# Moving the S5 units of a hybrid layer ahead, into the key/value projection

## The chip, the cores and the metric

The kernel runs on one core of a Trainium2 chip. The metric is device time in microseconds (us) from one execution of the whole program; the number quoted for a kernel is the median over its runs. The engines are named as the profile names them: PE (matrix multiply; PEld is its weight load), DVE (vector), ACT (scalar and activation), POOL (GpSimd), and SP, whose queue here issues nearly all loads. Each engine works through its own instructions in the order in which the program wrote them.

## The reference

Two layers of a diffusion backbone over 256 context and 256 latent tokens, width 1024. Each layer is a half-step SwiGLU, a token mixer, and a second half-step SwiGLU. The case is about the mixer of layer 0, which runs two head groups on the same input: a bidirectional S5 state-space group and a grouped-query attention group.

```python
def mixer_ab(hx, hc, ...):
    z = hx @ w_in
    u, q, k, v = jnp.split(z, [S5_WIDTH, S5_WIDTH + qw, S5_WIDTH + qw + kw], axis=-1)
    ...
    for r in range(2):                     # forward and reversed
        yl, yc = s5_direction(uc, u, ...)  # linear recurrence over tokens, then a read-out
        y_lat = y_lat + yl
    ...
    b_lat = dense_gqa(qn, kn, v, kcn, vch) # latent queries read 512 keys
    b_ctx = attend_full(qc, kcn, vch)      # context queries read 256 keys
    out_lat = jnp.concatenate([s5_glu(y_lat, glu_w), b_lat], axis=-1) @ w_out
```

## The kernel before

All matrix work is float32 by three products: a weight or activation is split into a high part (`whi`, `hh`: a cast) and a low part (`wlo`, `hl`: a subtraction), and `mm3` (lines 350 to 352) multiplies high by high, high by low and low by high. The split of a weight block is two casts on ACT (line 252) and two subtractions on DVE (line 258).

**Loads.** A list `plan` holds every weight block in the order of use. `fetch` issues them on the SP queue into a ring of three buffers `raw` of 1 MB. For a weight (`"w"`) the buffer is given back when its low part is written; for S5 data (`"s"`) when the S5 unit that reads it calls `done_raw`. Before the change the order around the mixer is: key/value weights `abkv`, the two halves of the query weights `abq`, then the S5 blocks `at` (input matrices, one for two units) and `me` (read-out matrices) in order of use. `u_load` brings the S5 input `U` back from DRAM in two halves of eight transfers each; `s5_tab` loads a unit's rotation table `tbl` (256 KB) into one of three buffers.

**The mixer (`mixer_ab`)** runs these stages on PE: the projection to S5 inputs (`puu`), four blocks of 128 tokens of keys and values (`pkv`, line 1575 on), four blocks of queries in two halves (`pq`), attention, then the output projection (`pwo`). After every piece of PE work the code calls `tick()`, which takes one step of each generator in the list `bg`: `k_gen` and `q_gen` finish a block of keys or queries (norm, rotary table, transposes), and `s5_gen` runs the events that are due at its tick number. Thus a tick number is a place in the order of every engine's instructions. Before the change `s5_gen` enters `bg` after the key/value blocks, so its tick 0 lies in the first half of query block 0.

**The S5 work** is eight units n = 0 to 7 (quad n // 2 and direction n % 2). A unit is issued at tick `S5_TICKS[n]`: 32 small matmuls `psS` on PE (line 1415) and a copy `Ssb` on ACT (line 1418; one buffer, `SB = 1`). One tick later come two rotations on POOL (lines 1443 to 1445, three operations of 128x256 each, then a copy `rhoT`), which read `Ssb` and `tbl`. Three and four ticks after the issue come two halves of the scan on DVE: two scans (line 1460), then products `pr` and `t` (1469, 1470) and the states `H` (1474); the second half has no scans. Six and seven ticks after the second unit of a quad come the two read-out halves `py` on PE (line 1492), and a tick later a copy `yt` on ACT.

**Attention** has 16 score steps, numbered 0 to 15 here; each is two heads of 128 queries, against 256 keys in steps 0 to 7 and 512 in steps 8 to 15. A step is the scores `sc` on PE, the row maximum `mx` on DVE (line 893), the exponentials `P` on ACT (line 913), scaling on ACT (928) and POOL (930), and three steps later transposes `ppt` and their copies (941); the products with the values `po` follow every second step. Each step is one tick.

Of the kernel before, what the change touches and what calls it, by code (L numbers as in the profile page):

```python
# [21 lines left out]
KT = D // 128  # L22
# [14 lines left out]
def hybrid_kernel(ctx: ExitStack, tc: tile.TileContext, x, c, ctx_in, c_ctx, mod_w, mod_b, norm_g, ffn_wg, ffn_wu,  # L37
# [6 lines left out]
    def pool(name, bufs=1, **kw):  # L44
        return ctx.enter_context(tc.tile_pool(name=name, bufs=bufs, **kw))

    S5_TICKS = (0, 3, 7, 9, 12, 15, 17, 19)
    S5_LAG = (0, 3, 4, 6)
    QL = (1, 2, 2, 2)
    FK = (0, 1, 3, 6)  # L50
# [34 lines left out]
    FL = (1, 3)  # L85
    SPL = (1, 1, 1, 1)
    LT = 0
    GT = 3
    GN = 1
    AH = 26  # L90
    KL = ((3, 7), (1, 2), (2, 3), (1, 1))
    PB = (8, 6)
    TBB = 3
    SB = 1
    ctx.enter_context(tc.manual_schedule())
# [88 lines left out]
    bg = []  # L184
# [78 lines left out]
    def lo_done(i):  # L263
        while lo_q and lo_q[0][0] <= i:
            lo_q.pop(0)[1]()
# [27 lines left out]
    def use(key, pre=True, mods=True):  # L293
        if mods:
            run_mods()
        while plan[st["cur"]][0] == "s":
            st["cur"] += 1
        i = st["cur"]
        assert plan[i][1] == key, (plan[i][1], key)
        fetch()  # L300
        prep(i)
        lo_done(i)
        st["cur"] += 1
        if pre:
            ahead()
        return prepped.pop(i)

    def w_spec(key, w, r0, nr, c0, ncol):
        plan.append(("w", key, nr, ncol, lambda rv: [
            (rv, w[r0:r0 + nr * 128, c0:c0 + ncol].rearrange("(k p) n -> p k n", p=128))]))  # L310
# [532 lines left out]
    def k_gen(ap, psrc, nh, l, t, kTh, kTl, tok, lag=(1, 1)):  # L843
# [8 lines left out]
        for i0 in range(0, nh, 2):  # L852
            hl = ap.tile([128, 2, 4, 64], F32R, name="khl", tag="P", bufs=PB[l])
            yy = y[:, i0:i0 + 2, None, :].to_broadcast([128, 2, 2, 64])
# [465 lines left out]
    def ab_specs():  # L1320
        w = ab_w_in[0]
        for i in range(2):
            w_spec(("abu", i), w, 0, KT, 256 * i, 256)
            for ch in (range(MA), range(MA, 4))[i]:
                m_spec(0, 6, ch)
        o = [(("abkv",), w, 0, KT, 1024, 256)]
        o += [(("abq", i), w, 512 * i, 4, 512, 512) for i in range(2)]
        for sp in o:
            w_spec(*sp)

        def at_spec(qd):
            plan.append(("s", ("at", qd), 2, 1024, lambda rv: [(rv, at_d[qd])]))

        def me_spec(i):
            plan.append(("s", ("me", i), 12, 128, lambda rv: [
                (rv.rearrange("p (f g) n -> p f (g n)", f=2),
                 me_d[i // 2][:, :, i % 2].rearrange("p f b z n -> p f (b z n)"))]))

        def mx_spec(ch):
            plan.append(("s", ("mx", ch), 8, 256, lambda rv: [  # L1340
                (rv, mod_w[0, :, 7 * D + ch * 256:7 * D + (ch + 1) * 256].rearrange("(k p) n -> p k n", p=128))]))

        uses = [(S5_TICKS[2 * qd], 0, at_spec, qd) for qd in range(4)]
        uses += [(S5_TICKS[2 * (i // 2) + 1] + S5_LAG[3] + i % 2, 1, me_spec, i) for i in range(8)]
        uses += [(t, 2, mx_spec, ch) for ch, t in enumerate(MX)]
        for _, _, f, i in sorted(uses, key=lambda u: u[:2]):
            f(i)
        def wo_spec(kh, ch):
            def srcs(rv, cs_=slice(ch * 512, (ch + 1) * 512)):
                if kh == 0:  # L1350
                    return [(rv, w_out[0, 0:512, cs_].rearrange("(k p) n -> p k n", p=128))]
                return [(rv[64 * kvl:64 * kvl + 64],
                         w_out[0, 512 + 256 * kvl:768 + 256 * kvl, cs_].rearrange("(k p) n -> p k n", p=64))
                        for kvl in range(2)]
            plan.append(("w", ("wo0", kh, ch), 4, 512, srcs))

        wo_spec(1, 0)
        def glu_srcs(z):
            return lambda rv: [(rv[64 * qe:64 * qe + 64, 2 * qp:2 * qp + 2],
                                glu_w[0, z, 256 * qp + 128 * qe:256 * qp + 128 * qe + 128].rearrange("(a f) n -> f a n", a=2))  # L1360
                               for qp in range(2) for qe in range(2)]

        for z in range(2):
            plan.append(("w", ("glu", z), 4, 512, glu_srcs(z)))
        wo_spec(0, 0)
        wo_spec(1, 1)
        wo_spec(0, 1)

    def mixer_ab(nm, ap, nxt):
# [33 lines left out]
        def s5_tab(n):  # L1403
            qd, r = divmod(n, 2)
            tb = ap.tile([128, 2, 4, 64], F32, name="tbl", tag="tbl", bufs=TBB)
            nc.sync.dma_start(tb, tab_d[r][:, :, qd * 256:(qd + 1) * 256].rearrange("p z (q c) -> p z q c", q=4))
            return tb
# [16 lines left out]
        s5 = {"tb": {}, "sb": {}, "uu": {}, "H": {}, "py": {}}  # L1424
# [71 lines left out]
        def s5_store(qd):  # L1496
            qp, qe = divmod(qd, 2)
            if qe == 0:
                tg_ = ("qhl", "tbl")[qp]
                s5["yt", qp] = [ap.tile([128, 4, 2, 64], F32, name="yt", tag=tg_, bufs=(2, TBB)[qp]) for _ in range(2)]  # L1500
            py = s5["py"].pop(qd).rearrange("p (s j h) -> p s j h", s=4, j=8)
            for jh in range(2):
                S.copy(s5["yt", qp][jh][:, :, qe].rearrange("p j (s h) -> p s j h", h=16), py[:, :, 4 * jh:4 * jh + 4])
# [23 lines left out]
        def at_tick(t, f, *a):  # L1527
            events.setdefault(t, []).append(lambda: f(*a))

        TU = S5_TICKS  # L1530
        o_ = S5_LAG
# [11 lines left out]
        for n in range(8):  # L1543
            at_tick(TU[n], s5_unit, n)
        for n in range(8):
            at_tick(max(0, TU[n] - 2), lambda n: s5["tb"].update({n: s5_tab(n)}), n)
        def mod_raw(ch):
            mod_chunk((0, 7, -1 - ch), use_raw(("mx", ch)))
            done_raw()

        for ch, t in enumerate(MX):
            at_tick(t, mod_raw, ch)
        at_tick(AH, ahead)
        tg = TU[7] + o_[3] + GT
        for k in range(4):
            at_tick(tg + k // GN, gelu, k // 2, k % 2)

        def s5_gen():
            for t in range(max(events) + 1):
                for f in events.get(t, []):  # L1560
                    f()
                yield
# [7 lines left out]
        kTh = ap.tile([128, 2, 512], F32R, name="kTh")  # L1570
        kTl = ap.tile([128, 2, 512], F32R, name="kTl")
        v = ap.tile([128, 4, 128], F32, name="v")
        qT = ap.tile([128, 8, 512], F32R, name="qT", tag="big")
        ckv = use(("abkv",))
        for t in range(4):
            tk = slice(t * 128, (t + 1) * 128)
            pkv = ps("pkv")
            for k in range(KT):
                s_, tl = tokens(t)
                mm3(pkv[:, 0:256], (hh[:, s_, k, tl], hl[:, s_, k, tl]), (ckv[0][:, k], ckv[1][:, k]), k == 0, k == KT - 1)  # L1580
            S.copy(v[:, t], pkv[:, 128:256])
            bg.append(k_gen(ap, pkv[:, 0:128], 2, 0, t - 2 if t >= 2 else None, kTh, kTl, tk))
            tick()
            if t == 1:
                u_load(1)
        sg_ = s5_gen()
        bg.append(sg_)
        rq = ap.tile([128, 4, 2, 8], F32, name="rq")
        cqs = {}
        for t in range(4):  # L1590
# [344 lines left out]
```

## Time and profile before

| | us |
|---|---|
| median of 3 runs | 1775.09 |
| lowest and highest | 1774.59, 1776.67 |
| the profiled execution | 1775.49 |
| its span, first to last instruction | 1773.7 |
| PE busy in the span | 1720.3 |
| DVE busy | 1051.9 |
| ACT busy | 633.3 |
| POOL busy | 447.3 |

The span is nearly the whole time; 1.8 us lie around it. Over the program PE is busy for 97%. Only a short part of the span holds the change: the key/value and query projections from 478.6 us, attention from 521 us, and the output projection from 609.7 us. What bounds this part is read from its own stretch and not from the sums above.

### The profile page before, as it was taken

What the parts mean: (1) busy time and instruction counts of PE and PEld (TensorE: products, weight loads), DVE (VectorE), ACT (ScalarE), POOL (GpSimd) and SP (SyncE); (2) the same over time, 40 slices, a digit from 0 to 9 for tenths busy, and PEclk for the clock granted to TensorE, in tenths of its full rate; (3) what the DMA queues carried; (4) which work ended last, traced back from release to release, by engine and by line L of the source; (5) the groups of instructions that cost most, each with busy time, mean ns of one, the idle gap of its engine ahead of it and who ended that gap; (6) DMA issues with size and microseconds to landing.
All of it is one profiled execution on the core that took longest, in us unless ns stands there. A gap on an engine that the chain in (4) does not pass through costs nothing.

```text
span 1773.7 us, 25534 instructions
## 1 busy us (share of the span) xinstructions
PE 1720.3 (97%) x10127; PEld 1433.3 (81%) x10127; DVE 1051.9 (59%) x1760; ACT 633.3 (36%) x1202; POOL 447.3 (25%) x601
## 2 busy tenths in 40 slices
PE   6999999999987999999999999999999998999998
PEld 4778878878975789888888888888888876699998
DVE  5566767665579644576653355765644468755555
ACT  3322222223446634222222233222222347754443
POOL 5314768322467304000000032000000146630000
PEclk8999999999998899999999999999999999999999
DMA  8546475585444524564433325553524244155653
GB/s 265 184 136 178 147 216 172 184 286 190 159 144 157 137 83 137 167 210 136 147 113 101 119 99 182 171 167 130 158 78 133 95 167 96 40 199 167 198 181 121
DMA packets 209247, 272.63 MB, mean 154 GB/s; under 512 B 23464, under 2 KB 171176, under 8 KB 208616
## 3 DMA queue, kind: packets, MB, share of 16 engines
q1 hardware_dynamic: 203632, 257.06, 46.1%
q10 hardware_dynamic: 4136, 9.52, 1.5%
q0 software_dynamic: 1360, 4.42, 0.8%
q8 instruction: 80, 1.31, 0.3%
q14 instruction: 39, 0.32, 0.1%
HBM read 255.77 MB, written 15.17 MB: 153 GB/s over the span
## 4 chain that ended last, share of the span: by engine, by line
PE 81%; DVE 7%; DMA 4%; POOL 3%; ACT 2%; issue 2%; SPq 0%; POOLq 0%; ACTq 0%
PE pu L350 15%; PE pu L351 15%; PE pu L352 15%; PE pd L350 6%; PE pd L352 6%; PE pd L351 6%; PE pwo L350 1%; PE pwo L352 1%; PE pwo L351 1%; PE pacc L351 1%; PE pacc L350 1%; PE pacc L352 1%; DMA me_d<-Et 1%; PE pm L411 1%; DVE H L1474 1%
## 5 line engine op out<-in xcount | busy, mean ns | idle before, releaser
L350 PE MATMUL pu<-hh,whi 128*128 128x512 f32 (+1 forms) x1472 | 528.2, 359 | 1.3 <-ACT hh L505 1.1
L351 PE MATMUL pu<-hl,whi 128*128 128x512 f32 (+1 forms) x1472 | 523.5, 356 | 3.5 <-DVE hl L507 2.6
L352 PE MATMUL pu<-hh,wlo 128*128 128x512 f32 (+1 forms) x1472 | 522.8, 355 | 0.1
L258 DVE TENSOR_TENSOR wlo<-raw,whi 128x1024 fp32r<-128x1024 f32 (+2 forms) x326 | 370.5, 1176 | 62.1 <-ACT whi L252 61.7
L252 ACT CAST whi<-raw 128x1024 fp32r<-128x1024 f32 (+2 forms) x330 | 308.3, 984 | 275.4 <-PE pd L351 158.9
L350 PEld LDWEIGHTS pu<-hh,whi 128*128 128x128 f32 x1472 | 278.4, 189 | 51.6 <-issue 6.8
L351 PEld LDWEIGHTS pu<-hl,whi 128*128 128x128 f32 x1472 | 278.5, 189 | 43.0 <-DVE hl L507 3.4
L352 PEld LDWEIGHTS pu<-hh,wlo 128*128 128x128 f32 x1472 | 278.4, 189 | 40.0 <-DVE wlo L258 0.7
L462 POOL TENSOR_TENSOR acc<-acc,sq 128x256 f32<-128x256 f32 x54 | 43.1, 801 | 774.7 <-ACT sq L468 773.8
L350 PE MATMUL pd<-ahi,whi 128*128 128x512 f32 (+1 forms) x624 | 224.8, 360 | 0.3 <-ACT ahi L217 0.3
L351 PE MATMUL pd<-alo,whi 128*128 128x512 f32 (+1 forms) x624 | 222.7, 357 | 0.5 <-DVE alo L218 0.5
L555 DVE TENSOR_TENSOR hm<-sg,pu 128x512 f32<-128x512 f32 (+1 forms) x88 | 54.4, 618 | 284.1 <-PE pu L352 284.1
L352 PE MATMUL pd<-ahi,wlo 128*128 128x512 f32 (+1 forms) x624 | 222.6, 357 | 0.0
L217 ACT CAST ahi<-hm 128x512 fp32r<-128x512 f32 (+1 forms) x88 | 49.9, 567 | 362.6 <-DVE hm L555 362.6
L546 DVE SCALAR_TENSOR_TENSOR xT<-pd,m,xT 128x256 f32<-128x256 f32 x192 | 84.5, 478 | 104.4 <-PE pd L352 104.2
L350 PEld LDWEIGHTS pd<-ahi,whi 128*128 128x128 f32 x624 | 117.9, 189 | 20.6 <-issue 2.9
L352 PEld LDWEIGHTS pd<-ahi,wlo 128*128 128x128 f32 x624 | 117.9, 189 | 17.5 <-DVE wlo L258 0.5
L351 PEld LDWEIGHTS pd<-alo,whi 128*128 128x128 f32 x624 | 118.0, 189 | 17.3 <-DVE alo L218 0.8
L551 ACT ACTIVATE sg<-pu 128x512 f32<-128x512 f32 (+1 forms) x88 | 47.6, 544 | 224.2 <-PE pu L352 223.7
L441 DVE SCALAR_TENSOR_TENSOR ma<-mraw,silc,ma 128x1024 f32<-128x1024 f32 (+1 forms) x112 | 123.7, 1145 | 6.4 <-DMA mraw<-in_mod_w_dram 6.4
L218 DVE TENSOR_TENSOR alo<-hm,ahi 128x512 fp32r<-128x512 f32 (+1 forms) x88 | 56.0, 636 | 56.7 <-ACT ahi L217 56.7
L505 ACT ACTIVATE hh<-h,m 128x256 fp32r<-128x256 f32 x88 | 41.2, 502 | 58.8 <-DVE h L498 58.8
(355 smaller groups left out, 2328.1 us busy)
## 6 DMA issues: line engine op xcount, KB each, us to landing
raw<-in_ffn_wg_dram SPq DMA_DIRECT2D x44, 1024.0 KB, 5.4
raw<-in_ffn_wu_dram SPq DMA_DIRECT2D x44, 1024.0 KB, 5.5
raw<-in_mod_w_dram SPq DMA_DIRECT2D x40, 1024.0 KB, 5.0
raw<-in_ffn_wd_dram SPq DMA_DIRECT2D x36, 768.0 KB, 4.9
mraw<-in_mod_w_dram SPq DMA_DIRECT2D x48, 512.0 KB, 4.7
raw<-in_ffn_wd_dram SPq DMA_DIRECT2D x17, 1024.0 KB, 5.0
raw<-me_d SPq DMA_DIRECT2D x8, 768.0 KB, 5.5
raw<-in_win_w_in_dram SPq DMA_DIRECT2D x6, 1024.0 KB, 5.3
```

The costliest lines, as they stand in the source:

```text
L217: (S.copy if eng is None else eng.tensor_copy)(dst_hi, src)
L218: V.tensor_sub(dst_lo, src, dst_hi.bitcast(F32))
L252: S.copy(v[0][:, js], raw[:, js])
L258: eng.tensor_sub(v[1][:, js], raw[:, js], v[0][:, js].bitcast(F32))
L350: T.matmul(o, lhs[0], rhs[0], start=start, stop=False)
L351: T.matmul(o, lhs[0], rhs[1], start=False, stop=False)
L352: T.matmul(o, lhs[1], rhs[0], start=False, stop=stop)
L441: V.scalar_tensor_tensor(ma[c0, s_], raw[i], silc[:, k, s_:s_ + 1], ma[c0, s_], op0=OP.mult, op1=OP.add)
L462: G.tensor_add(acc[s_], acc[s_], sq_late.pop(s_))
L546: V.scalar_tensor_tensor(xT[:, d, sl], psrc, m[:, l, j, d, s_:s_ + 1], xT[:, d, sl], op0=OP.mult, op1=OP.add)
L551: S.activation(sg, pg, AF.Silu)
L555: V.tensor_mul(hm, sg, pu)
```

## The change

The S5 generator enters `bg` ahead of the key/value blocks. Its ticks 0 to 3 now lie in these blocks, ticks 4 to 12 in and behind the query projections, and the score steps begin at tick 13. The units are issued at ticks 1, 2, 4, ..., 14, where the ticks of before (0 to 19), counted from the same place, were 4 to 23. `at(0)` is loaded ahead of the query weights. A table is loaded no earlier than the scan that frees its buffer (`TU[n - 3] + o_[2]`). The outputs `yt` of the first two quads get buffers of their own in place of those of `qhl`; to make room, the tiles `P` of attention are 6 and not 8. `GT` and `AH` move the start of the S5 read-out's activation (`gelu`) and of an early weight split; the first is written at the same place as before, at the first pieces of the output projection.

```diff
-    S5_TICKS = (0, 3, 7, 9, 12, 15, 17, 19)
+    S5_TICKS = (1, 2, 4, 6, 8, 10, 12, 14)
...
-    GT = 3
+    GT = 12
-    AH = 26
+    AH = 25
-    PB = (8, 6)
+    PB = (6, 6)
...
-        o = [(("abkv",), w, 0, KT, 1024, 256)]
-        o += [(("abq", i), w, 512 * i, 4, 512, 512) for i in range(2)]
-        for sp in o:
-            w_spec(*sp)
+        w_spec(("abkv",), w, 0, KT, 1024, 256)
...
-        for _, _, f, i in sorted(uses, key=lambda u: u[:2]):
+        for n, (_, _, f, i) in enumerate(sorted(uses, key=lambda u: u[:2])):
             f(i)
+            if n == 0:
+                for i in range(2):
+                    w_spec(("abq", i), w, 512 * i, 4, 512, 512)
...
-                tg_ = ("qhl", "tbl")[qp]
+                tg_ = ("yt", "tbl")[qp]
...
-            at_tick(max(0, TU[n] - 2), lambda n: s5["tb"].update({n: s5_tab(n)}), n)
+            at_tick(max(0, TU[n] - 2, TU[n - 3] + o_[2] if n > 2 else 0), lambda n: s5["tb"].update({n: s5_tab(n)}), n)
...
         ckv = use(("abkv",))
+        sg_ = s5_gen()
+        bg.append(sg_)
...
-            bg.append(k_gen(ap, pkv[:, 0:128], 2, 0, t - 2 if t >= 2 else None, kTh, kTl, tk))
+            bg.insert(bg.index(sg_), k_gen(ap, pkv[:, 0:128], 2, 0, t - 2 if t >= 2 else None, kTh, kTl, tk))
             tick()
             if t == 1:
                 u_load(1)
-        sg_ = s5_gen()
-        bg.append(sg_)
```

On the SP queue, at the loads around the first half of `U` (- is before, + is after; `in_ab_w_in_dram` is `abkv` in the form 128x8x256 and `abq` in the form 128x4x512):

```order
 L232 DMA raw<-in_ab_w_in_dram 128x8x256
-L232 DMA raw<-in_ab_w_in_dram 128x4x512
+L232 DMA raw<-at_d 128x2048
 L1400 DMA U<-u_d 16x16x64 x8
-L232 DMA raw<-in_ab_w_in_dram 128x4x512
-L232 DMA raw<-at_d 128x2048 x2
+L232 DMA raw<-in_ab_w_in_dram 128x4x512 x2
+L232 DMA raw<-at_d 128x2048
+L1406 DMA tbl<-tab_d 128x2x256 x2
 L1400 DMA U<-u_d 16x16x64 x8
```

The first `abq` block has moved behind `U`, and the first two tables have moved ahead of the second half of `U`, behind `at(1)`.

On ACT, in the key/value blocks, after the change (`hsq` squares of a key block, `v` its values, `kTh` and `kTl` the transposed keys, `whi` the split of a weight block, here of `abq`; the first row is `abq(0)`, the last `abq(1)`):

```order
L252 CAST whi<-raw 128x1024 x2
...
L1418 COPY Ssb<-psS 128x512
L1583 COPY v<-pkv 128x128
L866 CAST kTh<-pkt 128x2x128
L867 CAST kTl<-pkt 128x2x128
L803 ACTIVATE hsq,hss<-pkv 128x64 x2
L1418 COPY Ssb<-psS 128x512
...
L252 CAST whi<-raw 128x1024 x2
```

Two copies `Ssb`, of units 0 and 1, now stand between the two weight splits; before, none did.

On DVE, in attention before the change, around score steps 8 to 10:

```order
L893 TENSOR_REDUCE mx<-sc 128x1 x2
L905 TENSOR_TENSOR mx<-mx,rq 128x2
L925 RECIPROCAL smx<-smx 128x2
L954 CAST hh_102<-po 128x128
L955 TENSOR_TENSOR hl_104<-po,hh_102 128x128
L954 CAST hh_102<-po 128x128
L955 TENSOR_TENSOR hl_104<-po,hh_102 128x128
L1460 SCALAR_TENSOR_TENSOR uu<-rhoT,uu 128x256 x2
L1469 TENSOR_TENSOR pr<-uu,tbl 128x256
L1470 TENSOR_TENSOR t_5500<-uu,tbl 128x256
```

And after, from the end of unit 7's scan at score step 6 on:

```order
L893 TENSOR_REDUCE mx<-sc 128x1 x2
L905 TENSOR_TENSOR mx<-mx,rq 128x2
L925 RECIPROCAL smx<-smx 128x2
L893 TENSOR_REDUCE mx<-sc 128x1 x2
L905 TENSOR_TENSOR mx<-mx,rq 128x2
L925 RECIPROCAL smx<-smx 128x2
L954 CAST hh_102<-po 128x128
L955 TENSOR_TENSOR hl_104<-po,hh_102 128x128
L954 CAST hh_102<-po 128x128
L955 TENSOR_TENSOR hl_104<-po,hh_102 128x128
L893 TENSOR_REDUCE mx<-sc 128x1 x2
```

Before, scans stand among the maxima up to step 15, and units 0 to 3 are written ahead of the maximum of step 6; after, all eight units are, and no scan follows it.

## Rows read from the trace of the kernel before

**Rows 1.** Busy time of each engine (instructions), clock, DMA, by stretch (start:end, us).

```profile
478.60:509.20 30.60, 30.60 (x250) 27.51 (x247) 14.11 (x34) 14.68 (x68) 8.91 (x15) 1.00 0.75 222
509.20:552.80 43.60, 33.09 (x301) 26.08 (x301) 41.60 (x98) 20.62 (x80) 35.62 (x43) 0.84 0.30 99
552.80:598.00 45.20, 35.17 (x306) 26.04 (x302) 41.55 (x103) 28.49 (x73) 31.50 (x33) 0.88 0.44 129
598.00:609.70 11.70, 11.55 (x105) 8.69 (x103) 4.40 (x11) 9.82 (x19) 3.13 (x2) 0.86 0.57 133
```

**Rows 2.** Timeline of the SP queue (start us, us issuing, transfers), key/value stage.

```profile
481.08 4.28 SPq L1400 DMA_DIRECT2D U<-u_d  x8
485.46 0.39 SPq L232 DMA_DIRECT2D raw<-in_ab_w_in_dram  x1
```

**Rows 3.** Chain that ended last (start us, us, what): two transfers, issue to landing.

```profile
474.41 7.56 DMA raw<-in_ab_w_in_dram
...
498.67 5.62 DMA tbl<-tab_d
```

**Rows 4.** Timeline, ACT: the two splits of the query weights.

```profile
481.99 2.00 ACT L252 CAST whi<-raw 128x1024 fp32r<-128x1024 f32 x2 [3.90 <-DMA raw<-in_ab_w_in_dram]
...
492.41 2.02 ACT L252 CAST whi<-raw 128x1024 fp32r<-128x1024 f32 x2
```

**Rows 5.** Timeline, PE: first transposes of the keys.

```profile
487.54 0.60 PE L864 MATMUL pkt<-ident,khl 128*128 128x128 f32 x4
```

**Rows 6.** Timeline, POOL: first and last reading multiply of unit 0's rotation.

```profile
504.42 0.73 POOL L1443 TENSOR_TENSOR uu<-Ssb,tbl 128x256 f32<-128x256 f32 x1 [10.82 <-DMA tbl<-tab_d]
...
507.30 0.75 POOL L1444 TENSOR_TENSOR t<-Ssb,tbl 128x256 f32<-128x256 f32 x1
```

**Rows 7.** Timeline, DVE: low parts, first query block, scan of unit 0.

```profile
483.07 2.36 DVE L258 TENSOR_TENSOR wlo<-raw,whi 128x1024 fp32r<-128x1024 f32 x2 [0.92 <-ACT whi L252]
...
501.48 0.69 DVE L806 TENSOR_TENSOR hy<-pq,gains 128x512 f32<-128x512 f32 x1 [4.62 <-ACT hsq L803]
502.20 0.29 DVE L217 CAST qhl<-hy 128x256 fp32r<-128x256 f32 x1
...
509.23 1.27 DVE L1460 TENSOR_TENSOR_SCAN uu<-rhoT,uu 128x256 f32<-128x256 f32 x2 [0.70 <-POOL rhoT L1449]
...
511.19 0.84 DVE L1474 TENSOR_TENSOR H<-pr,t 64x252 f32<-64x252 f32 x2
```

**Rows 8.** Groups by line and form, DVE, 552.8 to 598 us: the scans.

```profile
L1460 DVE TENSOR_TENSOR_SCAN uu<-rhoT,uu 128x256 f32<-128x256 f32 x8 | 5.8, 765 | 0.3 <-POOL rhoT L1449 0.3
L1474 DVE TENSOR_TENSOR H<-pr,t 64x252 f32<-64x252 f32 x8 | 5.3, 666 | 0.2
L1470 DVE TENSOR_TENSOR t<-uu,tbl 128x256 f32<-128x256 f32 x8 | 5.1, 640 | 0.0
L1469 DVE TENSOR_TENSOR pr<-uu,tbl 128x256 f32<-128x256 f32 x8 | 4.4, 552 | 0.0
L1474 DVE TENSOR_TENSOR H<-pr,t 64x124 f32<-64x124 f32 x8 | 3.3, 409 | 0.2
...
L1474 DVE TENSOR_TENSOR H<-pr,t 64x128 f32<-64x128 f32 x8 | 2.4, 306 | 0.0
```

**Rows 9.** Timeline, ACT: first exponential of steps 5, 6, 12 and 13.

```profile
551.08 0.56 ACT L913 ACTIVATE P<-sc,mx,rq 128x256 f32<-128x256 f32 x1 [1.67 <-DVE smx L925]
...
553.26 0.57 ACT L913 ACTIVATE P<-sc,mx,rq 128x256 f32<-128x256 f32 x1
...
585.38 0.78 ACT L913 ACTIVATE P<-sc,mx,rq 128x512 f32<-128x512 f32 x1 [3.90 <-DVE smx L925]
...
589.01 0.78 ACT L913 ACTIVATE P<-sc,mx,rq 128x512 f32<-128x512 f32 x1 [0.42 <-DVE smx L925]
```

**Rows 10.** Chain that ended last, after the last exponential.

```profile
599.63 2.23 PE py L1492 x24
...
604.76 1.31 PE py L1492 x24
```

## The prediction

> **What bounds the kernel now.** The profiled execution took 1775.49 us. The change touches the stretch from the first key/value block (478.6 us) to the output projection (609.7 us), so I read that stretch by windows first [rows 1]. The windows are cut where the work changes hands: at 509.2 DVE starts the first S5 scan, at 552.8 it has finished the maximum of score step 6, at 598.0 the last exponential starts. Up to 509.2 PE is never idle (30.6 of 30.6 us) and DVE rests for 16.5 us (30.6 less 14.1). From 509.2 to 598.0 it is the other way round: DVE works 41.60 of 43.60 and 41.55 of 45.20 us, PE only about three quarters. So attention is bound by DVE, and ACT says the same: the exponentials of steps 5 and 12 each waited for a DVE result behind a scan [rows 9]. After 598.0 PE bounds again. S5 scans hold DVE for 26.3 us in the second window alone (5.8 + 5.3 + 5.1 + 4.4 + 3.3 + 2.4, units 4 to 7) [rows 8].
>
> That makes the question exact. Moving scans forward is worth something only if they run in the 16.5 idle us ahead of 509.2. If they start no earlier than now, the same DVE work follows in another order, and the time depends on whether DVE is kept as full.
>
> **When can the first scan start after the change?** I follow the loads. Now the first query block `abq(0)` is issued at 474.41 and lands 7.56 us later [rows 3], and ACT splits it from 481.99 [rows 4]. After, `at(0)` takes that place, and `abq(0)` stands behind the first half of `U`, whose issue takes SP from 481.08 to 485.36; the next load of a weight there is issued at 485.46 [rows 2]. That load now is `abq(1)`; its split starts at 492.41 with no wait for it [rows 4], so it takes at most 6.95 us. I give `abq(0)` that: landing at 492.4, bounds 491.1 (as fast as the smaller table, 5.62) [rows 3] and 493.0 (the 7.56). Everything that hangs on this split moves by some 10 us: the first keys' transposes, 5.55 us behind the start of the split now (481.99 to 487.54) [rows 4, 5], come at about 498. PE, which will have done three key blocks by 492, stands still there, as it does ahead of unit 0's matmuls, which need `U`, whose last transfer is issued at 485 only.
>
> The tables come next. They are queued behind `at(1)`, which needs the buffer of `abq(0)` and so its low part: now that ends 3.44 us behind the start of the split (481.99 to 485.43) [rows 4, 7], then at 495.8. With two issues in between, the table of unit 0 is issued at about 496.3, and at 5.62 us [rows 3] it lands at 501.9. Now it landed at 504.3. So the change, meant to start the units some 10 us earlier, brings the first rotation forward by only 2.4 us.
>
> Then comes a wait that is new. `Ssb` has one buffer. ACT's copy for unit 1 must wait until the rotation of unit 0 has read it, 3.63 us after the rotation starts (504.42 to 508.05) [rows 6], that is until 505.5. Behind this copy on ACT stand the values and squares of key block 3 and the split of `abq(1)`, and behind that, on DVE, its low part and the rest of key block 3. Copy 0.6, key work 1.4, first half of the split 1.0 (half of 2.02) [rows 4], low part 2.36 [rows 7], rest of the key block 1.1 (short operations; an estimate): 505.5 + 6.5 = 512.0. Unit 0's scan, written behind all this on DVE, starts at about 512 and not at 509.2: **+2.8 us**, bounds 0 and +4.
>
> **The sum over DVE.** From there I count DVE's work up to the maximum of step 6, at 552.8 now:
> - start: +2.8;
> - `hy` and the split of query block 0 and `hy` of block 1 lie ahead of the first scan now, behind its start then: two at 0.69 and four splits of which the first takes 0.29 and the pairs some 0.7 [rows 7]: +2.8;
> - units 4 to 7 lie ahead of step 6 instead of behind it: +26.3 [rows 8].
>
> Step 6's maximum is done 31.9 us later, at 584.7, if DVE is as full as now (2.0 us idle in 43.6). Its new neighbours are the rotations on POOL, written three ticks ahead, and the query squares on ACT; they gate the scans now as well.
>
> From step 6 on no scan is left. Steps of 256 keys follow each other by 2.2 us when no scan lies between (steps 5 and 6: 551.08, 553.26), those of 512 keys by 3.6 us (steps 12 and 13) [rows 9]; at that pace ACT and PE are nearly full, so I take it as the floor. Steps 6 to 15 then take 2 x 2.2 + 7 x 3.6 = 29.6 us, now 45.2 [rows 1]: **-15.6**. Behind the last exponential two pieces of the read-out leave PE's chain, 2.23 + 1.31 [rows 10]: **-3.5**.
>
> Sum: 2.8 + 2.8 + 26.3 - 15.6 - 3.5 = +12.8 us. One term is left, the price of a scan. Unit 0, whose scan met no rotation, took 2.80 us for the first half (509.23 to 512.03) [rows 7]; the second half is the same without the two scans of 1.2, 1.6 us. That is 4.4 a unit, where units 4 to 7 took 26.3 / 4 = 6.6. The difference comes from POOL: the same `H` operation takes 0.42 there and 0.67 in the mean of the later units [rows 7, 8]. After the change the rotations are packed closer around the scans, but the scaling of `P` on POOL no longer runs beside them. The bounds are 4.4 for all eight (-17.6 against 6.6) and a few us more than now. I take a relief of 2.8, nearest to 6.6, because the eight rotations still run beside DVE's work. Forecast: **+10 us**, 1785.5 against the profiled 1775.49, and 1785 against the median of 1775.09. `GT`, `PB` and the own tiles I cost at nothing: the activation of the read-out is written at the same place, with six `P` tiles an exponential waits for transposes that ACT's copies ahead of it wait for already, and the tiles take no engine time. Without that cover each would show as a wait of a fraction of a step.
>
> **Rivals.**
> - *The scans fill DVE's rest (faster).* Place: 478.6 to 509.2, with 16.5 us of idle DVE. If `abq(0)` lands as early as now and table 0 by about 490, up to 16.5 us of scans leave attention; less 4 us that PE and ACT then need, 1763. It decides at the landing of `abq(0)`: later than about 485, ACT and DVE have nothing to do ahead of it. The order on SP speaks against it. Chance 0.11.
> - *The scans cost their clean price (no change).* With most of the 17.6 us of relief the sum is near -5 to +5 and the time 1770 to 1778. For it: the scaling of `P` no longer competes. Against: rotations do. Chance 0.16.
> - *PE becomes the chain (slower still).* PE waits several times in the key blocks and at `abq(1)`. The granted clock was 1.00 up to 509.2, where PE never rested, and 0.84 where it was idle for 10.5 of 43.6 us [rows 1]. At 0.84 the 30 us of projections take 36; with the waits added, PE may reach attention after DVE does, +5 to +8 on my forecast: 1790 to 1793. Chance 0.15.
> - *Rotations hold up every scan (slowest).* With the rotations packed against the scans, each of a rotation's six operations could hold up a DVE operation for its whole 0.73 us [rows 6]: 4.4 on the clean 4.4, 8.8 a unit, 70 us for eight and not 53, +17 on my sum and 1802 or more. For it: the `H` means of 0.42 and 0.67. Against: the scans proper took 0.77 in the mean of units 4 to 7, against 0.64 in unit 0 [rows 7, 8], and rotations already ran beside the scans. Chance 0.05.
> - That the units are not moved is excluded by the order; how early they run is the first rival.
>
> The Trainium skill, SBUF — State Buffer, section Who interferes with whom, states the mechanism of the slowest rival as a rule: a DVE instruction with two SBUF inputs and a GpSimd instruction that reads SBUF block each other for a whole instruction. Taken alone it makes the time 1802; the `H` means agree with its direction, the scans hardly. The Trainium skill, Perfetto Trace Analysis, section Optimization Strategy, says of regimes bound by different engines that "performance may be improved by interleaving those regimes". It speaks against this change, which parts scans that were spread over attention; no row here gives it a time.
>
> **How the numbers follow.** The forecast has 0.53 (1779 to 1789). 0.2% of the time, 3.55 us, is about what a measurement of this kernel can tell from no change. Faster by more than that: 0.11, plus 0.01 of the second rival; within it: 0.15; slower: forecast and the two slower rivals, 0.73. The range 1771 to 1797 takes in the clean price at the lower end and the PE chain at the upper, and leaves out the first rival and the last.
>
> **What would show it.** In the changed profile: `abq(0)`'s split starting on ACT near 492; PE idle ahead of the first key transposes; ACT's second `Ssb` waiting on POOL; the first scan near 512; step 6's maximum near 582; then steps of 512 keys 3.6 us apart with DVE partly idle; `pwo` starting near 620. I am wrong if the first scan starts before 500, if a unit's scan costs DVE under 5 us, or if the free steps run well under 3.6 us.

## The result and the profile after

The changed kernel took 1790.93 us (median of 4 runs, 1789.81 to 1791.71), the kernel before beside it 1774.84 us: a ratio of 1.0088 with a 95% interval of 1.0071 to 1.0106. That is 16.1 us slower, where the forecast was 10 us slower. The profiled execution took 1790.84 us, 15.4 us over the one of before; the key/value blocks begin at 477.60 us there and at 478.58 before, so 1.0 us has to be added when a time of after is set against one of before.

Nearly all of the loss is there when the output projection starts: its first `pwo` matmul stands at 623.73, before at 609.69, which is 15.0 us later with that 1.0. Of the windows of after (answer to [rows 1]) the first two have the times of before, and the others are cut at events: 584.0 is a microsecond behind the maximum of score step 6, 612.7 just behind the start of the last step's first exponential (612.45), 623.8 the start of `pwo`. The columns are those of [rows 1].

```profile
478.60:509.20 30.60, 24.51 (x218) 22.02 (x218) 11.06 (x25) 9.10 (x32) 12.21 (x17) 0.85 0.76 216
509.20:552.80 43.60, 36.00 (x339) 29.10 (x338) 39.48 (x78) 15.28 (x80) 32.94 (x44) 0.91 0.45 140
552.80:584.00 31.20, 20.54 (x146) 14.40 (x148) 30.27 (x81) 14.37 (x47) 20.33 (x22) 0.75 0.43 118
584.00:612.70 28.70, 26.73 (x190) 17.82 (x186) 19.21 (x55) 27.05 (x67) 12.79 (x10) 0.97 0.40 111
612.70:623.80 11.10, 9.05 (x56) 5.12 (x54) 1.96 (x8) 7.76 (x16) 2.01 (x2) 0.85 0.00 0
```

Three things are to be seen. In the first window PE, which never rested before, rests for 6.1 us, and its granted clock is 0.85 where it was 1.00; DVE, which was to be filled there, does 11.06 us of work, less than the 14.11 of before. In the third DVE is full (30.27 of 31.20). In the fourth DVE works for 19.21 of 28.70 us, and ACT is the full engine (27.05): DVE's rest in front was not filled (16.5 us before, 19.5 now), and 9.5 us of rest lie beside the late steps as well.

ACT and PE show where the front went (timelines; answers to [rows 4, 5]).

```profile
490.01 1.99 ACT L252 CAST whi<-raw 128x1024 fp32r<-128x1024 f32 x2 [12.90 <-DMA raw<-in_ab_w_in_dram]
...
503.11 0.59 ACT L1418 COPY Ssb<-psS 128x512 f32<-128x512 f32 x1 [5.86 <-POOL t L1444]
```

```profile
487.33 1.98 PE L1415 MATMUL psS<-U,raw 128*64 128x64 f32 x32 [3.49 <-DMA U<-u_d]
...
524.79 1.94 PE L838 MATMUL pqt<-ident,qhl 128*128 128x128 f32 x8 [6.09 <-DVE qhl L218]
```

ACT stands still for 12.9 us, because the split of `abq(0)` is the next thing in its order and the weights have not come; the squares of the key blocks are written behind it. PE stands still for `U`, and later for the split of query block 0, which DVE now does between scans. Unit 0's scan starts here, on DVE (answer to [rows 7]):

```profile
505.79 2.90 DVE L258 TENSOR_TENSOR wlo<-raw,whi 128x1024 fp32r<-128x1024 f32 x2
...
512.88 1.27 DVE L1460 TENSOR_TENSOR_SCAN uu<-rhoT,uu 128x256 f32<-128x256 f32 x2 [1.78 <-POOL rhoT L1449]
...
582.33 0.76 DVE L893 TENSOR_REDUCE mx<-sc 128x1 f32<-128x256 f32 x2
```

The first scan stands at 512.88, 3.65 us later than before, or 4.6 us counted from the start of the key/value blocks (35.3 against 30.7), and the maximum of step 6 ends at 583.09. The scan's last wait is for POOL, and POOL's timeline says for which of its operations:

```profile
505.86 1.75 POOL L1443 TENSOR_TENSOR uu<-Ssb,tbl 128x256 f32<-128x256 f32 x1
507.57 1.71 POOL L1444 TENSOR_TENSOR t<-Ssb,tbl 128x256 f32<-128x256 f32 x1
...
512.46 0.39 POOL L1449 COPY rhoT<-rho 128x252 f32<-128x252 f32 x1
```

This is the rotation of unit 1. `rhoT`, which holds the decays that the scan multiplies by, is one tile, and with units 0 and 1 one tick apart the copy of unit 1 is written ahead of unit 0's scan. So the first scan waits for the second rotation, and it reads the decays of unit 1 and not its own. The order is the same in every kernel below with the two units at neighbouring ticks.

### The profile page after: what moved, and what is told of

Same layout as the page of the kernel before. It is cut to its first block, busy times and chain, and to the rows that moved or that the text cites. A ratio compares the mean times of both kernels' runs of the same rounds, so it can differ in the third digit from the quotient of the medians.

```text
span 1789.1 us, 25532 instructions
## 1 busy us (share of the span) xinstructions
PE 1727.6 (97%) x10127; PEld 1434.9 (80%) x10127; DVE 1052.7 (59%) x1760; ACT 632.7 (35%) x1202; POOL 449.3 (25%) x601
## 4 chain that ended last, share of the span: by engine, by line
PE 60%; DVE 4%; ACT 3%; issue 2%; POOL 1%; DMA 1%; POOLq 0%; ACTq 0%
PE pu L350 11%; PE pu L352 11%; PE pu L351 11%; PE pd L350 4%; PE pd L352 4%; PE pd L351 4%; PE pwo L350 1%; PE pwo L352 1%; PE pwo L351 1%; PE po L950 1%; PE pacc L350 1%; PE pacc L351 1%; PE pacc L352 1%; PE ppt L940 1%; ACT P L913 1%
```

## The experiments

All medians are from 4 to 11 runs, and each ratio is to the kernel before on the same chip. The kernel before took 1773.95 to 1774.84 us on these chips, so a difference between two of the medians below is good to about 1 us.

**The loads ahead of `U` (b1_uload).** The two query weight blocks are issued before `U` blocks the queue.

```diff
-        u_load(0)
         kTh = ap.tile([128, 2, 512], F32R, name="kTh")
...
         ckv = use(("abkv",))
+        u_load(0)
```

> The changed kernel with the first half of U loaded behind the line that takes the key/value weights, so that both query weight blocks are issued ahead of U, near 478 instead of 484.4. Theory A (the time is DVE's work counted from the first scan, and the first scan hangs on the loads): abq(0) lands near 485 to 486, its split on ACT starts there and not at 490.0, at(1) and the first tables are issued about 5 us earlier, the first scan starts near 505 instead of 512.9, and the whole time falls by 5 to 8 us, to 1783 to 1786. Rival B (PE, or ACT in the free steps, is the chain whatever DVE does): the first scan moves as well, but the time falls by less than 3 us.

Measured: 1791.73 us, 1.0093 (1.0078 to 1.0108). Theory A falls; rival B has the time, but its reason does not hold either, since the first scan did not move. The weights came, as expected, at 485.36; but the eight transfers of `U`, now behind 2 MB of weights, took 7.51 us to issue instead of 3.78 (the queue of SP), and PE waits 6.73 us for them instead of 3.49:

```profile
481.49 7.51 SPq L1400 DMA_DIRECT2D U<-u_d  x8
```

```profile
491.68 1.98 PE L1415 MATMUL psS<-U,raw 128*64 128x64 f32 x32 [6.73 <-DMA U<-u_d]
```

The first scan starts 35.9 us behind the first key/value matmul (514.61 less 478.73), in the changed kernel 35.3. A wait for weights was exchanged for a wait for `U`.

**And the first tables (b2_utab).** As b1, with `s5_tab(0)` and `s5_tab(1)` ahead of `u_load(0)`.

> As the run before it, with the tables of units 0 and 1 issued ahead of U too, near 478.5. Theory A: the tables land by 486, unit 0's rotation starts as soon as its Ssb is copied (near 490 instead of 499.5), the first scan near 498 to 500, and the time falls by 11 to 14 us against the changed kernel, to 1777 to 1780, since 12 us of scans now run in DVE's rest ahead of the attention. Rival B: the scans start early but the time stays within 4 us of the run before it, since in their new place they hold up the key and query blocks, which PE waits for.

Measured: 1792.43 us, 1.0098 (1.0083 to 1.0113). PE's wait for `U` is 8.32 us, the granted clock 0.67 from 490 to 500, and the first scan stands at 514.53. Theory A falls again, and rival B has the time but not the early scans. With the tables there by then, unit 0's rotation still starts only at 500.86: on POOL it is written behind the squares' sums of a key block, which waits for PE.

**The old places of the units, the new loads (b3_spread), and the new loads alone (b4_at0).**

```diff
 b3, against the changed kernel
-    S5_TICKS = (1, 2, 4, 6, 8, 10, 12, 14)
+    S5_TICKS = (4, 7, 11, 13, 16, 19, 21, 23)
-    GT = 12
+    GT = 3
-    AH = 25
+    AH = 30
 b4, against the kernel before: only the order of the plan, at(0) ahead of abq
```

> The changed kernel with everything but the front-loading: generator from the key/value blocks on, load order, table rule and own output tiles stay, but the units are issued at ticks 4, 7, 11, 13, 16, 19, 21, 23, the places of before. Theory A (what costs is that no scan is left for the ACT-bound steps behind step 6): the scans lie between the exponentials again, and the time goes back to 1775 to 1780, the rest being the later first scan. Rival C (the load order, at(0) ahead of the query weights, is what costs): 1786 to 1791.

> The kernel before with one edit: at(0) loaded ahead of the query weights. Theory A: PE stands still a few us ahead of the first query block, DVE's first scan starts 0 to 4 us later, and the time is 1775 to 1779. Rival C (the load order is the cause): 1786 or more.

Measured: b3 1785.57 us, 1.0058 (1.0042 to 1.0075); b4 1785.41 us, 1.0058 (1.0043 to 1.0073). Theory A falls, and rival C, whose ranges began at 1786, is right for 11 of the 16 us: one 1 MB load placed ahead of the query weights costs 11 us on the kernel before, with nothing else changed. The rows of b4 (ACT, PE and DVE):

```profile
490.53 1.99 ACT L252 CAST whi<-raw 128x1024 fp32r<-128x1024 f32 x2 [12.22 <-DMA raw<-in_ab_w_in_dram]
```

```profile
495.66 1.36 PE L864 MATMUL pkt<-ident,khl 128*128 128x128 f32 x4 [7.75 <-DVE khl L855]
```

```profile
519.63 1.26 DVE L1460 TENSOR_TENSOR_SCAN uu<-rhoT,uu 128x256 f32<-128x256 f32 x2
```

ACT waits 12.2 us for the weights with the key blocks' squares behind, PE waits 7.75 us for the keys, which need these squares, and the first scan comes 10.4 us later than before. The whole delay reaches the end.

From here on theory D was: 11 us from the loads, about 5 from the missing scans beside the late steps.

**Front-loading with the old first load (f1_front).**

```diff
         w_spec(("abkv",), w, 0, KT, 1024, 256)
+        w_spec(("abq", 0), w, 0, 4, 512, 512)
...
             if n == 0:
-                for i in range(2):
-                    w_spec(("abq", i), w, 512 * i, 4, 512, 512)
+                w_spec(("abq", 1), w, 512, 4, 512, 512)
...
-    S5_TICKS = (1, 2, 4, 6, 8, 10, 12, 14)
+    S5_TICKS = (3, 4, 6, 8, 10, 12, 14, 16)
-    GT = 12
+    GT = 10
```

> The changed kernel with abq(0) loaded first again, then at(0), then abq(1), and the units two ticks later (3, 4, 6, 8, 10, 12, 14, 16), so that no S5 matmul stands on PE in front of a key/value block. Theory D (the loss of the changed kernel is two things: about 10 us because PE stands still ahead of the queries, for U or for abq(0), as at(0) ahead of the query weights alone cost; and about 5 us because no scan is left beside the steps behind step 6): PE has no wait over 2 us up to 510, the first scan starts at 498 to 503, and the time is 1776 to 1781. Rival E (the first stall is not the matter: scans packed together cost so much more that front-loading loses whatever the loads do): 1785 or more. Rival F (scans fill DVE's rest, the first rival of the prediction): 1763 to 1769.

Measured: 1778.61 us, 1.0027 (1.0016 to 1.0037). The time is where D put it. PE is nearly whole again in the first window, as before:

```profile
478.60:509.20 30.60, 29.98 (x269) 26.63 (x269) 15.99 (x37) 13.70 (x55) 15.26 (x24) 1.00 0.80 252
```

The first scan, at 507.64, is later than I wrote; it stands behind the split of query block 0. From it to `pwo` f1 takes 105.9 us, the kernel before 100.5: with `abq(0)` first again, 5.5 us are lost behind a first scan that is 1.2 us earlier from the start of the key/value blocks. Front-loading is not the only difference that is left: `abq(1)` still stands behind `at(0)`, and the next run shows a part that has nothing to do with it.

**What is left of the change (f4_qspread).** Both query blocks ahead of `at(0)`, units at the old places.

> The changed kernel with both query weight blocks loaded ahead of at(0), as before, and the units at the places of before (4, 7, 11, 13, 16, 19, 21, 23). What is left of the change is the table rule, the own output tiles, six P tiles and the generator that starts early. Theory D: these cost nothing, 1774 to 1776. Rival: six P tiles or the own tiles cost a wait per step, 1778 or more.

Measured: 1775.76 us, 1.0014 (1.0005 to 1.0024). The table rule, the own tiles and six `P` tiles cost some 2 us, between 1 and 4 by the interval. Against b3, which differs in the load order alone, f4 is 9.8 us faster. And f1, with the front-loading, is 2.9 us slower than f4.

**No rotations (f7_norot).**

```diff
-            G.tensor_mul(scan_order(u_), chunk_order(sb[:, z], r), scan_order(co))
-            G.tensor_mul(scan_order(t2), chunk_order(sb[:, 1 - z], r), scan_order(si))
-            (G.tensor_sub if z else G.tensor_add)(u_, u_, t2)
+            G.memset(u_, 0.0)
```

> The changed kernel with the three operations of each half of a rotation on POOL replaced by one fill with zeros; the rotation is left out, the scans and all else stay. It measures what rotations beside scans cost. Theory D: DVE's S5 operations of the eight units fall from 50 us to 36 to 42 in all, Ssb is free at once, so the stall on ACT goes too, and the time falls by 8 to 14 us, to 1777 to 1783. Rival G (DVE's price is its own, or is set by what else reads SBUF): the S5 operations stay within 3 us of 50, and the time falls by less than 5.

Measured: 1775.00 us, 1.0009 (1.0000 to 1.0019), 15.9 us less than the changed kernel and so more than the 8 to 14 of theory D; D's sum of the S5 operations holds, and rival G falls. Groups by line, DVE, all eight units: before (509.2 to 598 us), after (512 to 583), and without rotations (495 to 578, line numbers 3 lower):

```profile
L1474 DVE TENSOR_TENSOR H<-pr,t 64x252 f32<-64x252 f32 (+2 forms) x48 | 21.3, 470 | 0.9
...
L1460 DVE TENSOR_TENSOR_SCAN uu<-rhoT,uu 128x256 f32<-128x256 f32 x16 | 10.8, 719 | 1.3 <-POOL rhoT L1449 1.3
L1470 DVE TENSOR_TENSOR t<-uu,tbl 128x256 f32<-128x256 f32 x16 | 9.0, 562 | 0.0
L1469 DVE TENSOR_TENSOR pr<-uu,tbl 128x256 f32<-128x256 f32 x16 | 8.5, 532 | 0.0
```

```profile
L1474 DVE TENSOR_TENSOR H<-pr,t 64x252 f32<-64x252 f32 (+2 forms) x48 | 19.5, 432 | 0.8
L1460 DVE TENSOR_TENSOR_SCAN uu<-rhoT,uu 128x256 f32<-128x256 f32 x16 | 13.7, 898 | 1.8 <-POOL rhoT L1449 1.8
L1470 DVE TENSOR_TENSOR t<-uu,tbl 128x256 f32<-128x256 f32 x16 | 8.8, 551 | 0.0
L1469 DVE TENSOR_TENSOR pr<-uu,tbl 128x256 f32<-128x256 f32 x16 | 8.3, 519 | 0.0
```

```profile
L1471 DVE TENSOR_TENSOR H<-pr,t 64x252 f32<-64x252 f32 (+2 forms) x48 | 14.7, 332 | 0.8
L1457 DVE TENSOR_TENSOR_SCAN uu<-rhoT,uu 128x256 f32<-128x256 f32 x16 | 10.1, 673 | 0.0
...
L1467 DVE TENSOR_TENSOR t<-uu,tbl 128x256 f32<-128x256 f32 x16 | 7.7, 479 | 0.0
L1466 DVE TENSOR_TENSOR pr<-uu,tbl 128x256 f32<-128x256 f32 x16 | 6.8, 426 | 0.0
```

The sums of the four S5 lines are 49.6, 50.3 and 39.3 us. In the changed kernel the rotations cost DVE 11.0 us, 1.4 a unit, and the change took nothing off the price of before: what the `H` operations gained, the scans proper lost. The start counts too: the first scan stands at 505.55, 6.8 us earlier from the start of the key/value blocks. Together that is 17.8 us, a little over the whole gain. No run leaves the rotations out of the kernel before, whose scans pay nearly the same; so f7 shows what rotations cost, and not that they are the loss.

**The last read-out back at the end (f8_tail).**

```diff
-            t1 = TU[2 * q + 1]
+            t1 = TU[2 * q + 1] + 9 * (q == 3)
```

> The changed kernel with the read-out of the last quad moved back by nine ticks, to the place of before, between the last transposes. By the prediction's term for the end (-3.5 us, all of it taken off PE's chain) the time rises by 3.5 us, to 1794. By what the changed trace suggests (PE waits 1.9 us there for ACT, and works at a lower clock behind that wait): by 0 to 1 us, 1791 to 1792.

Measured: 1786.85 us, 1.0079 (1.0062 to 1.0096), 4.1 us less than the changed kernel: both expectations had the sign wrong. About 1 us lies ahead of the edit (the first scan, from the start of the key/value blocks). Some 1.8 us come where the read-out was taken away. ACT's exponentials of steps 7 and 9, after and then f8:

```profile
585.41 0.59 ACT L913 ACTIVATE P<-sc,mx,rq 128x256 f32<-128x256 f32 x1
...
592.00 0.78 ACT L913 ACTIVATE P<-sc,mx,rq 128x512 f32<-128x512 f32 x1 [0.27 <-DVE smx L925]
```

```profile
584.15 0.59 ACT L913 ACTIVATE P<-sc,mx,rq 128x256 f32<-128x256 f32 x1
...
588.96 0.80 ACT L913 ACTIVATE P<-sc,mx,rq 128x512 f32<-128x512 f32 x1
```

6.59 us after, 4.81 in f8: at its new place the read-out stands between two scores on PE, and ACT, just becoming the full engine, waits for these scores. And at the end, where it is put back, it adds nothing against the profiled execution of the changed kernel. PE there, after, f8, and then b1, which like the changed kernel has no read-out there:

```profile
615.39 1.32 PE L940 MATMUL ppt<-ident,P 128*128 128x128 f32 x8 [1.90 <-ACT hh L941]
616.64 3.47 PE L950 MATMUL po<-hh,v 128*64 128x256 f32 x16
```

```profile
611.86 1.21 PE L940 MATMUL ppt<-ident,P 128*128 128x128 f32 x8 [0.44 <-ACT hh L941]
612.99 1.95 PE L950 MATMUL po<-hh,v 128*64 128x256 f32 x16
```

```profile
618.32 1.21 PE L940 MATMUL ppt<-ident,P 128*128 128x128 f32 x8 [1.90 <-ACT hh L941]
619.46 1.95 PE L950 MATMUL po<-hh,v 128*64 128x256 f32 x16
```

With the read-out PE waits 0.44 us for ACT, without it 1.90 us. After, the same 16 matmuls then take 3.47 us instead of 1.95: the window from 612.7 on has a granted clock of 0.85, in f8 the same stretch (608.9 to 619.9) has 1.00. From the last step's first exponential to `pwo`: 11.28 us after, 10.97 in f8. But the wait alone does not bring the low clock: in b1 it is as long, the 16 matmuls take 1.95, and the stretch is 9.64 us (9.65 in f7). Against these the read-out at the end costs 1.3 us, where the prediction had 3.5.

**Two `Ssb` buffers (e_sb2).** `SB = 2`, and five `P` tiles for the room.

> The changed kernel with two buffers for Ssb (and five P tiles instead of six, for the room). By the prediction's step that ACT's second Ssb holds up the split of abq(1) and all behind it until POOL has read the first: the copy comes near 500 instead of 503.1, the first scan near 509, and the time falls by 3 us, to 1787 to 1788.5. If the wait lies beside others that end as late (PE at its low clock, the transposes of the keys): the first scan moves by less than 1.5 us and the time by less than 1.

Measured: 1790.81 us, 1.0098 (1.0080 to 1.0115). The second copy stands at 496.40 without a wait, and the scan all the same at 511.31 with 2.47 us of waiting for `rhoT`; measured from the start of the key/value blocks it is 0.7 us earlier, as the second expectation had it. The wait for `Ssb` was real and lay beside the one for unit 1's rotation.

**Trying for the rest in front (g2_tabs, g3_mix).** g2 is f1 with the first two tables ahead of `U` and the last read-out back at the end (+7 ticks); g3 is g2 with `S5_TICKS = (3, 4, 8, 11, 14, 17, 19, 21)`.

> The run f1_front with two more edits: the tables of units 0 and 1 issued ahead of U, and the read-out of the last quad back between the last transposes. If the first rival of the prediction holds once the loads allow it (scans fill DVE's rest between 497 and 507, which in f1_front waits for a table that takes 12.5 us to land): unit 0's rotation starts near 493, the first scan near 498 to 500 instead of 507.6, and the time is 1766 to 1771, faster than before. If the early scans hold up the split of abq(1) or the key blocks instead: 1774 to 1778.

> As g2_tabs, but only units 0 and 1 stand early (ticks 3 and 4); the others are spread over attention nearly as before (8, 11, 14, 17, 19, 21). If DVE's work is the bound and its rest is worth the same wherever it is filled: DVE is kept full ahead of the queries and beside the exponentials too, 1765 to 1770, some 1 to 3 us below g2_tabs. If a scan beside the exponentials costs as much as the rest that it fills: the same as g2_tabs within 1 us or slower.

Measured: g2 1778.75 us, 1.0021 (1.0012 to 1.0031); g3 1778.05 us, 1.0019 (1.0010 to 1.0029). Neither gains on f1; g3, within 1 us of g2, is what its second expectation said, and g2 is just over the 1774 to 1778 of its own. In g2 unit 0's rotation does start at 493.40, but the scan is written behind the split of query block 0 and starts at 506.04. And both have, as f1 has, a wait on PE, here g2's, for the split of a query block that stands behind scans on DVE; before, no such wait was over 0.4 us, but PE waited as long for the states `H` (the second row shown), so the new wait is not shown to be the loss:

```profile
540.53 1.94 PE L838 MATMUL pqt<-ident,qhl 128*128 128x128 f32 x8 [5.65 <-DVE qhl L218]
```

```profile
528.04 0.70 PE L1492 MATMUL py<-raw,H 128*64 128x128 f32 x4 [5.76 <-DVE H L1474]
```

**One scan into one gap (h_early).** The kernel before, with edits for unit 0 alone.

```diff
+        s5["tb"][0] = s5_tab(0)
         u_load(0)
...
-        for n in range(8):
+        for n in range(1, 8):
             at_tick(max(0, TU[n] - 2), lambda n: s5["tb"].update({n: s5_tab(n)}), n)
...
-                at_tick(TU[n] + o_[1 + z], s5_scan, n, z)
+                at_tick(TU[n] + o_[1 + z] - (n == 0), s5_scan, n, z)
```

> The kernel before with two edits for unit 0 alone: its table is issued ahead of U, and its scan is written one tick earlier, so that the first half falls into the 4.2 us in which DVE waits for the squares of query block 1. If DVE's rest ahead of attention can be filled at all where the loads and the order allow it (the mechanism of the prediction's first rival): the first scan starts near 503.6 instead of 509.2, and the time falls by 2.8 to 4 us, to 1770 to 1772. If what is filled there comes back as a wait of PE for a later query split, as the other early runs showed: within 1.5 us of before.

Measured: 1771.56 us, 0.9982 (0.9973 to 0.9991): 3.1 us faster than the kernel before, and the fastest kernel of the study. DVE there, and then the last of these operations before:

```profile
502.31 1.26 DVE L1460 TENSOR_TENSOR_SCAN uu<-rhoT,uu 128x256 f32<-128x256 f32 x2
...
506.60 0.69 DVE L806 TENSOR_TENSOR hy<-pq,gains 128x512 f32<-128x512 f32 x1 [1.50 <-ACT hsq L803]
```

```profile
507.83 0.69 DVE L806 TENSOR_TENSOR hy<-pq,gains 128x512 f32<-128x512 f32 x1 [4.21 <-ACT hsq L803]
```

The wait for the squares of query block 1, 4.21 us before, is 1.50 us now, and the 2.8 us in between are the first half of unit 0's scan [rows 7]. Nothing waits longer for it: PE's wait for `H` is 3.14 us there (5.76 before), and none for a query split is over 0.4. The first expectation holds, for the scan and its earlier table together.

## Why the prediction was right, and where its sum was not

*Direction and place: right.* 1790.93 us lies in the range and on the slower side, and most of what the text said would show it did: `abq(0)`'s split at 490.0 (said: near 492), PE idle (for `U` after two key blocks, not three), the second `Ssb` waiting on POOL, the first scan at 512.88 (512), the maximum of step 6 ending at 583.09 (582), DVE partly idle behind it; with the 1.0 us, the scan and the maximum lie some 2 us behind what was said. `pwo` started at 623.73, not near 620, and the free steps were 3.1 us apart and not 3.6, towards one of the signs of being wrong that the text named.

*The sum, term by term* (times of after plus 1.0 us for the earlier start). Up to step 6: 584.1 against 581.9 in the sum. Most of these 2.2 us are the start: the first scan came 4.6 us later and not 2.8, beyond the bound of 4. From it to the maximum of step 6 went 70.2 us, where the sum has 69.9 with the relief, and that agreement is luck. The relief of 2.8 us on the scan price did not come (50.3 us for all eight units against 49.6 before, in the rows of f7). DVE idled 3.2 us there and not 2.0. Against that, the query blocks, booked at +2.8, cost nothing in sum: all of DVE's work that is not S5 took 16.7 us in this stretch, before 17.6, for the query split got cheaper. Its subtractions, before and then after (groups by line, DVE; a mean of 0.43 us also in f7, without rotations):

```profile
L218 DVE TENSOR_TENSOR qhl<-hy,qhl 128x256 fp32r<-128x256 f32 x6 | 3.9, 654 | 0.2
```

```profile
L218 DVE TENSOR_TENSOR qhl<-hy,qhl 128x256 fp32r<-128x256 f32 x8 | 3.4, 425 | 0.3
```

And the 26.3 for units 4 to 7 adds up overlapping operations; counted like the 49.6 they are 25.7.

Steps 6 to 15: 29.4 us (583.09 to 612.45) against 29.6. They were 3.1 us apart, not 3.6, but step 8 came late and an early weight split stood among them: `AH`, which the text did not cost, had moved it there from behind the last exponential, and steps 12 and 13, with the split at 603.47 between them, are 4.97 us apart (601.33 and 606.30). Again two errors cancel.

The end: 11.28 us against 8.2, since the term of -3.5 us failed. The text took the read-out's time off PE's chain and did not see that PE would then wait for ACT; in the profiled execution it also ran at the lower clock behind that wait, for 1.5 of the missing 3.1 us. By f8 and b1 the read-out is worth 0 to 1.3 us at the end, and it costs 1.8 at its new place. 2.2 - 0.2 + 3.1 = 5.1 us, and that is the distance from the forecast's +10 to the profile's +15.4 but for 0.3.

*The weight of the causes was not in the sum.* It charged the load order with 2.8 us, the delay of the first scan. b4 shows that the load order alone costs 11 us on the kernel before, with the first scan 10.4 us later. In the changed kernel the first scan is only 4.6 us late, and still f1, with `abq(0)` first again and the units two ticks later, is 12.3 us faster: 5.9 us ahead of the first scan, and 4.9 between it and `pwo` (105.9 against 110.9). So the loads are 10 to 12 of the 16.1 us. The 4.7 us that f1 keeps are about 1.8 of the change's other edits (f4) and 2.9 of front-loading, with `abq(1)` behind `at(0)` and the move of `AH` in it; what in those 2.9 us costs the time was not taken apart. Theory D's reason, that no scan is left beside the late steps, is not shown: g3 has scans there and gains nothing clear of noise. The prediction's count of DVE work gave a near total by another route, and that would have misled anyone who asked which edit to undo. That the forecast came out 6 us short and not further off is in part luck.

*The first scan was right for partly the wrong reason.* The text let it wait for `Ssb`, the split of `abq(1)` and its low part. Unit 0's rotation began at 499.45 and not at 501.9, and the second `Ssb` at 503.11 and not at 505.5; from there to the scan went 9.8 us and not 6.5. DVE was done with the key block at 511.10, after operations that ran slower beside unit 1's rotation, and waited for `rhoT`. With `Ssb` doubled (e_sb2) it moved by 0.7 us only, for the copy of `rhoT` of unit 1 ends as late. That single tile was not weighed.

*The rivals.* The scans do not fill DVE's rest in the changed kernel: its DVE does less ahead of 509.2 than before. The mechanism is real all the same: h_early fills 2.8 us of it. The clean scan price is 39.3 / 8 = 4.9 us a unit (f7; taken as 4.4 there), and with the rotations as near as before it is not reached. The rival of PE gave 1790 to 1793, and the time fell there, with its signs in the first window (6.1 us idle, clock 0.85); but from 512.9 to 584.1 DVE was busy for 68.0 of 71.2 us, so PE's delay acted through the start of the scans and not as a chain in attention. The slowest rival, 8.8 us a unit, is out: 6.3 were measured. (Its +17 gives 1802 from the forecast; from the sum of +12.8, which it names, it would be 1805.)

*The pages.* The Trainium skill, SBUF — State Buffer, section Who interferes with whom, has a DVE instruction with two SBUF inputs and a GpSimd instruction that reads SBUF block each other for a whole instruction. Single rows agree: beside the low part on DVE, whose two operations took 2.90 us instead of 2.36, POOL's reads took 1.75 and 1.71 us instead of 0.73. Over the eight units the price was 1.4 us each, not 4.4; how many operations met was not counted. The Trainium skill, Perfetto Trace Analysis, section Optimization Strategy, on interleaving regimes, spoke against the change. f1, which parts them and is 2.9 us slower than f4, agrees in direction; g3, which spreads six of the eight units over attention again, is no faster than f1 by more than 0.6 us, so no run shows that the parting costs the time.

## What to carry to other kernels

A load moved ahead in a queue is paid by everything that an in-order engine has written behind the wait for the load it displaced; follow that wait through all engines, not only to the operation one means to speed up. Work moved into idle time gains only where a named gap in the engine's own order takes it and nobody waits for what is written behind: one scan in one gap gave 3.1 us, eight units moved as a block stayed 4.7 us behind the kernel before even with the first query load back in its place. And matmuls that fill PE's wait for another engine are not to be booked in full as savings when they go: 1.3 us at most, of 3.5.

## What had not been expected of the hardware

A group of small transfers issued behind 2 MB of weights took twice as long to issue (7.51 us instead of 3.78 for the eight of `U`), so that two earlier loads made a later one late by about as much. The kernel before already showed it: its second half of `U`, issued at 486.93 behind three loads of 1 MB, took 10.99 us to issue. And after a rest of 1.90 us and eight transposes, PE's next 16 matmuls took 3.47 us instead of 1.95 in the changed kernel, without a wait of their own, and 3.32 in b2; in b1 and f7 the same rest was followed by 1.95. What makes the difference is not shown.
